# Two GpSimd sums for the first FFN's gate vector are written into the first mixer's second half

## The chip, the cores and the metric

The kernel runs on one core of one Trainium2 chip. The metric is the device time of one execution in microseconds (us); with several runs, their median. The engines are TensorE (PE, matrix products; PEld is its weight load), VectorE (DVE), ScalarE (ACT), GpSimd (POOL) and SyncE (SP, which here issues the loads). Each works through its own queue in order and waits on semaphores for the others.

## The reference

Two layers on 512 tokens of 1024 values. Layer 0 mixes tokens with HGRN2, layer 1 with dilated attention; behind each mixer stands a SwiGLU FFN with 2816 inner columns. Six vectors per layer, computed from the condition c, scale, shift and gate:

```python
cond = jax.nn.silu(c)
for layer in range(DEPTH):
    mod = (cond @ ada_w[layer] + ada_b[layer])[:, None, :]
    sh1, sc1, g1, sh2, sc2, g2 = jnp.split(mod, 6, axis=-1)
    u = rms_norm(h, norm_g[layer, 0]) * (1.0 + sc1) + sh1
    y = hgrn2_mixer(u, ...) if layer % 2 == 0 else dilated_attention_mixer(u, ...)
    h = h + (1.0 + g1) * rms_norm(y, norm_g[layer, 1])
    u = rms_norm(h, norm_g[layer, 2]) * (1.0 + sc2) + sh2
    y = swiglu_ffn(u, ffn_w_in[layer], ffn_w_out[layer])
    h = h + (1.0 + g2) * rms_norm(y, norm_g[layer, 3])
```

The change concerns g2 of layer 0, called (0, 5) in the kernel: 1024 sums over 1024 products of cond and ada_w.

## The kernel before, in words

All large products are computed in float32 as three products of rounded parts: an operand is split into a high part (ACT, `hi`, `oh`, `uh`) and a low part (the rest, DVE or POOL, `lo`, `ol`, `ul`), and L419 to L421 multiply high by high, low by high and high by low into a PSUM bank (`three`).

**The stream of loads.** A list `items` holds every weight tile in the order of use, and between them the pieces of the six vectors. `Stream` loads them with SP into two rotating places (`raw`), and `process_to` and `pieces` (L70 to L107) split weight tiles into `hi` and `lo`. An item of the kind "do" loads nothing; its function is called when the stream comes to it.

**The gate vector (0, 5).** Its four load items stand among the four tiles of the first mixer's output weights (`early`, L363). For each half of 512 columns DVE multiplies the rows by cond and adds them up partition by partition into a place in `shared` (L243, L245, `ada_chunk`). What remains is a sum over the 128 partitions that leaves the result on all of them. POOL does it with `partition_all_reduce`; for (0, 5) that is L254 in `reduce_both`, a "do" item behind the third tile of the FFN's input weights (L366). Then `row_fin` (L299, L300) adds the bias and multiplies by the norm's weights into `gate`, which is read at the very end of the FFN.

**Where the order comes from.** Inside `with tc.manual_schedule` the engines take their instructions in the order in which they are written. Outside of it a scheduler with a timeline model orders them. The "do" item is processed outside, so the scheduler chose its place: both sums stand in POOL's queue among the last two heads of the HGRN2 mixer, each ahead of an `orr`.

**The end of the HGRN2 mixer.** For each of 8 heads, `core_c` computes the head's output on PE, ACT squares and sums it (`oss`), DVE adds a constant (`rv`, L436), POOL takes the power -0.5 (`orr`, L437), and DVE scales the head with it (`aT`, L1438). `core_d` transposes it on PE (`ps_a`, L1445, four matmuls), ACT copies it out (`oT_late`, L1446), and DVE multiplies it by the mixer's gate (L1456). `mixer_out` then splits it (`cut`, L415 and L416) and multiplies it by the output weights: first columns 0 to 511 for all four token tiles (banks `ps_mm`, heads 0 to 7 in turn), then columns 512 to 1023 one token tile at a time (banks `ps_a`). All this is still ordered by the scheduler for layer 0.

**The second half of `mixer_out`** is written out by hand. Per token tile: squares of y (L457), the reciprocal root on POOL (`rr`, L472), the update of h, the norm, transposes (L502), the FFN's input u (`u_of`) and its two parts (`parts_of`, L519 and L520; the low part mostly on POOL). The last of them is `n.parts_of(3, 1, dve)`. Meanwhile PE multiplies the early tokens by the first FFN weights (`half`), and then the late ones (L691, L694).

**Then `ffn(0)`.** DVE builds sums over tokens (L732 to L739), PE multiplies the next column block, and `seven_products` computes two column blocks at a time with seven quarter products. It loads quarters of the weights, splits three of them (`spare` for the even steps, `hiq`/`loq` for others, L767 and L771), adds quarters (L775 on POOL, L779 and L783 on DVE) and splits the sums (L791 and L795). The first quarter loads go to the two places that the gate's bias and norm rows leave free when L300 has read them.

Of the kernel before, what the change touches and what calls it, by code (L numbers as in the profile page):

```python
# [15 lines left out]
P = 128  # L16
# [135 lines left out]
def block_kernel(tc, x, c, positions, ada_w, ada_b, norm_g, hgrn_w_in, lower, hgrn_norm_g, hgrn_w_out,  # L152
                 attn_w_in, attn_w_out, ffn_w_in, ffn_w_out, inv_freq, out):
    nc = tc.nc
    act, dve, pool, pe = nc.scalar, nc.vector, nc.gpsimd, nc.tensor
# [3 lines left out]
    with ExitStack() as ctx:  # L159
# [10 lines left out]
        def fresh(p, shape, tag, bufs=1, dt=F32):  # L170
            uid[0] += 1
            return p.tile(shape, dt, name=f"{tag}{uid[0]}", tag=tag, bufs=bufs)
# [30 lines left out]
        accs = {}  # L203
# [45 lines left out]

        def reduce_both(l, v):  # L250

            def run(_):
                for hf in range(2):
                    pool.partition_all_reduce(accs[l, v, hf], accs[l, v, hf], P, bass.bass_isa.ReduceOp.add)  # L254
            return ("do", None, run)

        def ada_item(l, v, hf, kq):
            src = ada_w[l, kq * 512:(kq + 1) * 512, v * D + hf * 512:v * D + (hf + 1) * 512]
# [82 lines left out]
        items = []  # L341
# [21 lines left out]
        early = [ada_item(0, 5, hf, kq) for hf in range(2) for kq in range(2)]  # L363
        items += hg_o[:2] + early[:2] + hg_o[2:3] + early[2:] + hg_o[3:]
        f0a, f0b = ffn_ws(0)
        items += f0a[:3] + [reduce_both(0, 5)] + f0a[3:4] + [fin_item(0, 5, 0), fin_item(0, 5, 1)] + f0a[4:]  # L366
        items += weave(f0b[:9], ada_seq((1, 1), (1, 0)), 0, 0.9) + f0b[9:]
        AW = attn_w_in[0]

# [44 lines left out]
        def split(hi, lo, src):  # L414
            act.copy(hi, src)  # L415
            dve.tensor_sub(lo, src, hi.bitcast(F32))  # L416
# [109 lines left out]
        def mixer_out(oT, otp, groups, gate, l, side, close, tail=None):  # L526


            aux = ExitStack()
            oh, ol = [], []  # L530

            def parts(n):
                uid[0] += 1
                pp = aux.enter_context(tc.tile_pool(name=f"parts{uid[0]}", bufs=1, side=bass.opposite_side(side)))
                place = not oh
                for _ in range(n):
                    oh.append(fresh(pp, [P, S], f"oh{len(oh)}", 1, F32R))
                if place:
                    pp.tile([P, 72], F32, name=f"pad{uid[0]}")

            def cut(kt):
                ol.append(fresh(otp, [P, S], *(("oT", 7) if kt < 7 else ("oT_late", 2)), F32R))
                split(oh[kt], ol[kt], oT[kt])

            parts(groups[0])
            y0 = [bank("mm") for _ in range(NT)]
            y1 = {}

            def prods(y, t, kt, w):
                tok = slice(t * P, (t + 1) * P)  # L550
                c = slice((kt % 4) * 512, (kt % 4 + 1) * 512)
                three(y, oh[kt][:, tok], ol[kt][:, tok], w[0][:, c], w[1][:, c], kt == 0, kt == KT - 1)

            def mm(t, kts):
                if t not in y1:
                    y1[t] = bank("a")
                for kt in kts:
                    prods(y1[t], t, kt, ws[kt // 4])

            if tail is None:  # L560
                for kt in range(KT):
                    if kt % 4 == 0:
                        w = st.take()
                    cut(kt)
                    for t in range(NT):
                        prods(y0[t], t, kt, w)
                ws = [st.take(1), st.take(0)]
            else:
                with tc.manual_schedule(engines=ORDERED):
                    for kt in range(3):  # L570
                        cut(kt)
                    for kt in range(KT):
                        if kt % 4 == 0:
                            w = st.take(0)
                        if kt == KT - 1:
                            ws = [st.take(0), st.take(0)]
                            mm(0, range(7))
                        for t in range(NT):
                            prods(y0[t], t, kt, w)
                        if kt == 0:  # L580
                            for fn in tail[-1]:
                                fn()
                            parts(groups[1])
                        if kt < 4:
                            cut(kt + 3)
                        for fn in tail.get(kt, ()):
                            fn()
                        if kt == 6:
                            cut(7)
                        if kt in (4, 5):  # L590
                            for hi_f, lo_f in st.pieces(2, True):
                                hi_f()
                                lo_f()
                            st.fill()
            close()
            n = Turn(side, y0, y1, gate, (l, 1))

            with tc.manual_schedule(engines=ORDERED):
                (hi_a, lo_a), (hi_b, lo_b) = st.pieces(2)
                n.sq_y(0, 0)  # L600
                n.gated(0, 0)
                mm(0, range(8) if tail is None else (7,))
                n.sq_y(0, 1)
                n.gated(0, 1)
                n.r_y(0)
                n.sq_y(1, 0)
                n.gated(1, 0)
                n.sq_y(2, 0)
                n.upds(0)
                n.sq_y(3, 0)  # L610
                n.gated(2, 0)
                n.r_h(0)
                hi_a()
                n.xn(0)
                mm(1, range(8))
                n.sq_y(1, 1)
                n.gated(1, 1)
                n.r_y(1)
                n.gated(3, 0)
                hi_b()  # L620
                n.upds(1)
                lo_a()
                mm(2, range(4))
                n.flip(0, [bank("b"), bank("b")])
                n.u_of(0, 0)
                n.r_h(1)
                n.u_of(0, 1)
                n.parts_of(0, 0)
                n.xn(1)
                n.parts_of(0, 1)  # L630
                lo_b()
                st.fill()
                mm(3, range(4))
                (hi_a, lo_a), (hi_b, lo_b) = st.pieces(2)
                mm(2, range(4, 6))
                n.flip(1, [bank("b"), bank("b")])
                n.u_of(1, 0)
                n.u_of(1, 1)
                n.parts_of(1, 0)
                n.parts_of(1, 1, dve)  # L640
                mm(2, range(6, 8))
                n.sq_y(2, 1)
                n.gated(2, 1)
                n.r_y(2)
                hi_a()
                n.upd(2, 0)
                mm(3, range(4, 8))
                n.sq_y(3, 1)
                n.sq_h(2, 0)
                n.upd(2, 1)  # L650
                n.sq_h(2, 1)
                hi_b()
                n.gated(3, 1)
                n.r_y(3)
                n.r_h(2)
                lo_a()
                n.xn(2)
                fw = [st.take(0), st.take(0)]
                pss = [bank("mm") for _ in range(4)]

                def half(i, tok):
                    block(*fw[i // 2], (i % 2) * P, 256, pss[i], tok, fu)
                half(0, EARLY)
                half(1, EARLY)
                n.flip(2, [bank("b"), bank("b")])
                n.upds(3)
                n.u_of(2, 0)
                n.u_of(2, 1, (0, 1))
                n.r_h(3)
                n.u_of(2, 1, (2, 3))  # L670
                n.xn(3)
                n.parts_of(2, 0)
                n.parts_of(2, 1)
                lo_b()
                st.fill()
                half(2, EARLY)
                n.flip(3, [bank("b"), bank("b")])
                n.u_of(3, 0)
                n.u_of(3, 1)
                n.parts_of(3, 0)  # L680
                n.parts_of(3, 1, dve)
                half(3, EARLY)
                for hi_f, lo_f in st.pieces(2):
                    hi_f()
                    lo_f()
                st.fill()
                tok = LATE
                for kt in range(KT):
                    a = kt * 256
                    for m, w in enumerate(fw[0]):  # L690
                        pe.matmul(pss[0][:, tok], w[:, a:a + P], fuh[kt // 4][:, kt % 4, tok], start=kt + m == 0, stop=False)  # L691
                for kt in range(KT):
                    a = kt * 256
                    pe.matmul(pss[0][:, tok], fw[0][0][:, a:a + P], ful[kt // 4][:, kt % 4, tok], start=False, stop=kt == KT - 1)  # L694
                for i in range(1, 4):
                    half(i, LATE)
            aux.close()
            return pss
# [1060 lines left out]
```

## Time and profile before

| | |
|---|---|
| median of 3 runs | 1526.21 us (1524.55 to 1527.09) |
| the profiled execution | 1527.45 us |
| its span in the profile | 1525.7 us |
| PE busy | 1502.3 us, 98% |
| DVE busy | 1033.1 us, 68% |
| ACT busy | 694.2 us, 45% |
| POOL busy | 240.6 us, 16% |
| mean granted clock of PE | 0.993 |
| L254 on POOL (the two sums) | 2 instructions of 3.25 us |

Times in rows are microseconds from the start of the span; a row of a timeline gives start, duration, engine, line, operation, output and inputs, and in brackets how long the engine stood idle before it and what it waited for. A wait put down to "issue" is one for which no semaphore accounts. The granted clock is the share of full speed at which PE ran in a stretch.

### The profile page before, as it was taken

To read this page: it belongs to the slowest core of one execution; us is meant where nothing else is said; L and a number is where in the kernel's file an instruction comes from. 1 tells how busy PE (TensorE), PEld (TensorE's weight loads), DVE (VectorE), ACT (ScalarE), POOL (GpSimd) and SP (SyncE) were. 2 spreads that over 40 slices of the span, in tenths; PEclk is the share of its full clock that TensorE was granted. 3 is DMA by queue.
4 is the path that set the end of the run, shared out by engine and by line. 5 is a ranking of instruction groups with operands and counts; after the bars stand their busy time and mean duration, and the time that the engine had idled before them with its cause. 6 is when DMAs were issued, how large, how long until landed. Compare 5 with 4: busy or idle time off the path is not lost.

```text
span 1525.7 us, 23115 instructions
## 1 busy us (share of the span) xinstructions
PE 1502.3 (98%) x9111; PEld 1327.7 (87%) x9111; DVE 1033.1 (68%) x1764; ACT 694.2 (45%) x1107; POOL 240.6 (16%) x212
## 2 busy tenths in 40 slices
PE   8999999899999999999999999999999999999998
PEld 6777888689999988889888888988888999999886
DVE  4577767478888897473557686345656978888633
ACT  4443433174444443363366655236555634454231
POOL 1011211130222211040010111000002212221100
PEclk9999999899999999999999999999999999999999
DMA  9553444313343356415544533443202233334531
GB/s 305 160 185 127 161 141 166 111 56 111 111 111 111 111 186 235 140 54 149 154 126 125 139 111 111 138 111 84 84 29 83 84 104 107 107 107 158 194 110 56
DMA packets 207645, 192.83 MB, mean 126 GB/s; under 512 B 6776, under 2 KB 166704, under 8 KB 207536
## 3 DMA queue, kind: packets, MB, share of 16 engines
q1 hardware_dynamic: 206000, 190.87, 40.6%
q8 instruction: 71, 1.16, 0.3%
q0 software_dynamic: 1024, 0.13, 0.2%
q10 hardware_dynamic: 512, 0.35, 0.1%
q14 instruction: 38, 0.31, 0.1%
HBM read 189.17 MB, written 2.16 MB: 125 GB/s over the span
## 4 chain that ended last, share of the span: by engine, by line
PE 89%; issue 3%; DVE 3%; DMA 2%; ACT 2%; POOL 1%; POOLq 0%; DVEq 0%; ACTq 0%
PE ps_mm L419 19%; PE ps_mm L421 19%; PE ps_mm L420 19%; PE ps_b L419 3%; PE ps_b L420 3%; PE ps_b L421 3%; PE ps_a L419 3%; PE ps_a L420 3%; PE ps_a L421 3%; PE ps_mm L1165 2%; DMA raw<-in_ada_w_dram 1%; PE ps_a L1165 1%; PE ps_a L1610 1%; PE ps_a L1592 1%; PE ps_mm L223 1%
## 5 line engine op out<-in xcount | busy, mean ns | idle before, releaser
L419 PE MATMUL ps_mm<-uh,hi 128*128 128x512 f32 (+1 forms) x784 | 290.0, 370 | 0.0
L421 PE MATMUL ps_mm<-uh,lo 128*128 128x512 f32 (+1 forms) x784 | 288.7, 368 | 0.0
L420 PE MATMUL ps_mm<-ul,hi 128*128 128x512 f32 (+1 forms) x784 | 287.5, 367 | 0.0
L85 DVE TENSOR_TENSOR lo<-raw,hi 128x2048 fp32r<-128x2048 f32 x74 | 177.4, 2397 | 158.5 <-ACT hi L84 158.5
L84 ACT CAST hi<-raw 128x2048 fp32r<-128x2048 f32 x74 | 141.2, 1908 | 143.8 <-DMA raw<-in_ffn_w_out_dram 49.7
L419 PEld LDWEIGHTS ps_mm<-uh,hi 128*128 128x128 f32 x784 | 147.4, 188 | 31.6 <-issue 8.4
L421 PEld LDWEIGHTS ps_mm<-uh,lo 128*128 128x128 f32 x784 | 147.7, 188 | 23.4
L420 PEld LDWEIGHTS ps_mm<-ul,hi 128*128 128x128 f32 x784 | 147.5, 188 | 22.7
L791 ACT CAST hiq<-raw 128x1024 fp32r<-128x1024 f32 x72 | 72.3, 1051 | 72.1 <-DVE raw L779 70.7
L419 PE MATMUL ps_mm<-hi,oh 128*128 128x512 f32 x240 | 94.1, 392 | 0.0
L420 PE MATMUL ps_mm<-lo,oh 128*128 128x512 f32 x240 | 93.5, 390 | 0.0
L245 DVE SCALAR_TENSOR_TENSOR shared<-raw,cond,shared 128x512 f32<-128x512 f32 x98 | 73.3, 748 | 25.6 <-DMA raw<-in_ada_w_dram 23.9
L795 DVE TENSOR_TENSOR loq<-raw,hiq 128x1024 fp32r<-128x1024 f32 x72 | 84.9, 1218 | 0.0
L247 POOL PARTITION_ALL_REDUCE shared<-shared x12 | 39.9, 3322 | 239.6 <-DVE shared L245 239.6
L421 PE MATMUL ps_mm<-hi,ul 128*128 128x512 f32 x192 | 76.0, 396 | 0.0
L775 POOL TENSOR_TENSOR raw<-raw 128x512 f32<-128x512 f32 x36 | 57.9, 1607 | 114.6 <-DVE loq L771 45.7
L420 PE MATMUL ps_mm<-lo,uh 128*128 128x512 f32 x192 | 75.9, 395 | 0.0
L419 PE MATMUL ps_mm<-hi,uh 128*128 128x512 f32 x192 | 74.6, 396 | 0.0
L779 DVE TENSOR_TENSOR raw<-raw 128x1024 f32<-128x1024 f32 x36 | 44.1, 1225 | 40.9 <-POOL raw L775 40.9
L421 PE MATMUL ps_mm<-hi,ol 128*128 128x512 f32 x176 | 68.5, 389 | 0.0
L419 PE MATMUL ps_a<-hi,oh 128*128 128x512 f32 x152 | 60.7, 400 | 0.0
L825 POOL TENSOR_TENSOR shared<-shared 128x256 f32<-128x256 f32 x36 | 27.7, 768 | 206.3 <-DVE shared L824 206.3
(403 smaller groups left out, 3939.6 us busy)
## 6 DMA issues: line engine op xcount, KB each, us to landing
raw<-in_ada_w_dram SPq DMA_DIRECT2D x40, 1024.0 KB, 5.1
raw<-in_ffn_w_in_dram SPq DMA_DIRECT2D x144, 256.0 KB, 4.2
raw<-in_attn_w_in_dram SPq DMA_DIRECT2D x48, 512.0 KB, 5.2
raw<-in_ffn_w_out_dram SPq DMA_DIRECT2D x22, 1024.0 KB, 4.9
raw<-in_hgrn_w_in_dram SPq DMA_DIRECT2D x12, 1024.0 KB, 5.5
raw<-in_attn_w_in_dram SPq DMA_DIRECT2D x12, 1024.0 KB, 5.0
raw<-in_ffn_w_in_dram SPq DMA_DIRECT2D x8, 1024.0 KB, 5.0
first<-in_ada_w_dram SPq DMA_DIRECT2D x14, 512.0 KB, 7.4
```

What stands on the lines that cost most here:

```text
L84: self.nc.scalar.copy(hi, t)
L85: self.nc.vector.tensor_sub(lo, t, hi.bitcast(F32))
L245: dve.scalar_tensor_tensor(a, r[:, k], sc, a, op0=OP.mult, op1=OP.add)
L247: pool.partition_all_reduce(a, a, P, bass.bass_isa.ReduceOp.add)
L419: pe.matmul(ps, ah, bh, start=start, stop=False)
L420: pe.matmul(ps, ah, bl, start=False, stop=False)
L421: pe.matmul(ps, al, bh, start=False, stop=stop)
L775: pool.tensor_add(r[:, 2], r[:, 2], r[:, 0])
L779: dve.tensor_tensor(r[:, 0:2], r[:, 0:3:2], r[:, 1:2].broadcast_to((P, 2, 512)), op=OP.add)
L791: act.copy(hi, src)
L795: dve.tensor_sub(lo, src, hi.bitcast(F32))
L1165: pe.matmul(vbanks[hf, t], a, w, start=e == 0 and which == 0, stop=e == KT - 1 and which == 2)
```

## The change

`reduce_both` no longer returns a "do" item but issues its two sums at once, and it is called inside the hand-written second half of `mixer_out`, behind `n.parts_of(3, 1, dve)`; the condition holds in layer 0 alone. The item leaves the list of loads. The same sums are computed on the same data.

```diff
         def reduce_both(l, v):
 
-            def run(_):
-                for hf in range(2):
-                    pool.partition_all_reduce(accs[l, v, hf], accs[l, v, hf], P, bass.bass_isa.ReduceOp.add)
-            return ("do", None, run)
+            for hf in range(2):
+                pool.partition_all_reduce(accs[l, v, hf], accs[l, v, hf], P, bass.bass_isa.ReduceOp.add)
...
-        items += f0a[:3] + [reduce_both(0, 5)] + f0a[3:4] + [fin_item(0, 5, 0), fin_item(0, 5, 1)] + f0a[4:]
+        items += f0a[:4] + [fin_item(0, 5, 0), fin_item(0, 5, 1)] + f0a[4:]
...
                 n.parts_of(3, 0)
                 n.parts_of(3, 1, dve)
+                if (l, 5, 1) in accs:
+                    reduce_both(l, 5)
                 half(3, EARLY)
```

The instructions of each engine stay the same in number, but for POOL, which has 4 changes of configuration around the two sums before and 2 now. Apart from the names' numbers the order changes on POOL, and, by the scheduler, at the end of the HGRN2 mixer on DVE and PE. SP's and ACT's orders stay.

POOL at the end of the HGRN2 mixer, before (`ISA shared` is a sum, `ISA` alone a change of configuration, `rr` the first root of the mixer's second half):

```order
L1387 TENSOR_TENSOR q_2129<-qd_2107,fpre_2113 128x512
L254 ISA
L254 ISA shared<-shared 128x512
L437 ISA
L437 TENSOR_TENSOR orr_2297<-rv_2298,expo 128x4
L254 ISA
L254 ISA shared<-shared 128x512
L437 ISA
L437 TENSOR_TENSOR orr_2331<-rv_2332,expo 128x4
L472 TENSOR_TENSOR rr_2564<-rv_2562,expo 128x1
```

POOL at the change from `mixer_out` to the FFN, now (line numbers of the changed file; `ul` is the last low part, `raw` the first sum of weight quarters):

```order
L518 TENSOR_TENSOR ul<-u_2904,uh 128x4x128
L253 ISA
L253 ISA shared<-shared 128x512 x2
L775 ISA
L775 TENSOR_TENSOR raw_3098<-raw_3098 128x512
```

Both sums have gone from ahead of the two orr to between ul and the first raw, where nothing stood before; the two orr now follow q directly.

DVE at the last head of the HGRN2 mixer, before and now (`lo` is the low part of the last tile of output weights, `aT` the scaled last head):

```order
L416 TENSOR_TENSOR oT_2491<-oT_late_689,oh_2358 128x512
L85 TENSOR_TENSOR lo_2456<-raw_2447,hi_2455 128x2048
L1438 TENSOR_TENSOR aT_2325<-ps_b_2317,orr_2331 128x512
L1456 TENSOR_TENSOR oT_late_690<-oT_late_690,Q_2280 128x512
```

```order
L414 TENSOR_TENSOR oT_2491<-oT_late_689,oh_2358 128x512
L1438 TENSOR_TENSOR aT_2325<-ps_b_2317,orr_2331 128x512
L85 TENSOR_TENSOR lo_2456<-raw_2447,hi_2455 128x2048
L1456 TENSOR_TENSOR oT_late_690<-oT_late_690,Q_2280 128x512
```

The scaled head has moved ahead of the low part.

PE at the same place, before and now (`ident,aT` are the four transposes; the rows with oh_2358 belong to head 6; the banks ps_mm hold columns 0 to 511, ps_a_2533 the other columns of the first token tile):

```order
L420 MATMUL ps_mm_2364<-lo_2189,oh_2358 128x512
L421 MATMUL ps_mm_2364<-hi_2188,oT_2491 128x512
L1445 MATMUL ps_a_2336<-ident,aT_2325 128x128 x4
L419 MATMUL ps_a_2533<-hi_2377,oh_2352 128x512
L420 MATMUL ps_a_2533<-lo_2378,oh_2352 128x512
```

```order
L417 MATMUL ps_mm_2361<-hi_2188,oh_2358 128x512
L418 MATMUL ps_mm_2361<-lo_2189,oh_2358 128x512
L1445 MATMUL ps_a_2336<-ident,aT_2325 128x128 x4
L419 MATMUL ps_mm_2361<-hi_2188,oT_2491 128x512
L417 MATMUL ps_mm_2362<-hi_2188,oh_2358 128x512
```

The transposes have moved ten matmuls ahead, into the products of head 6. Behind them now come 10 matmuls to ps_mm and 19 to ps_a_2533, and then the first product with the last head; before, it was 21 to ps_a_2533.

## The prediction

> **What bounds the kernel now.** I read the page first, then the waits of TensorE (PE), then the chain of waits around the place where the two sums over partitions run, then the timelines of GpSimd (POOL), VectorE (DVE) and PE there, and last the stretch into which the sums move.
>
> ```profile
> span 1525.7 us, 23115 instructions
> PE 1502.3 (98%) x9111; PEld 1327.7 (87%) x9111; DVE 1033.1 (68%) x1764; ACT 694.2 (45%) x1107; POOL 240.6 (16%) x212
> ```
>
> PE is busy for 98% of the span, so the time is PE's work plus the few moments in which it stands still. An edit on GpSimd can change the time only if it removes or makes such a moment. The waits of PE name the longest:
>
> ```profile
> PE ps_a L1445 <- DVE aT L1438: 6.3, 1, 6.3
> PE ps_b L502 <- DVE xn L496: 2.5, 2, 1.6
> ```
>
> It is one wait of 6.3 us: the transposes of the last head (L1445) wait for DVE's scaled head aT (L1438). The chain of waits says what DVE waited for:
>
> ```profile
> 278.34 0.75 DVE shared L245
> 279.10 0.61 DVE oT_late L1456
> 279.73 0.63 ACT oh L415
> 280.38 0.70 DVE oT L416
> 281.08 0.81 issue
> 281.89 3.25 POOL shared L254
> 285.22 7.26 issue
> 292.48 1.06 POOL orr L437
> 293.56 0.70 DVE aT L1438
> 294.31 1.12 PE ps_a L1445 x4
> ```
>
> DVE's aT needs the factor orr, which POOL computes in 1.06 us (L437). Ahead of it in POOL's queue stands one of the sums (L254), and between the sum's end and orr lie 7.26 us in which no semaphore is waited for. POOL's timeline, and the entries of its sequencer for L437 and L254, show what those are:
>
> ```profile
> 260.32 3.25 POOL L254 PARTITION_ALL_REDUCE shared<-shared  x1 [21.98 <-DVE shared L245]
> 272.12 1.06 POOL L437 TENSOR_TENSOR orr<-rv,expo 128x4 f32<-128x4 f32 x1 [8.55 <-DVE rv L436]
> 281.89 3.25 POOL L254 PARTITION_ALL_REDUCE shared<-shared  x1 [8.70 <-DVE oT L416]
> 292.48 1.05 POOL L437 TENSOR_TENSOR orr<-rv,expo 128x4 f32<-128x4 f32 x1 [7.34 <-issue]
> ```
> ```profile
> L254 POOLq MODIFY_POOL_CONFIG  x4: 9/10/11, 238.3 to 273.4; - x4
> L437 POOLq MODIFY_POOL_CONFIG  x4: 98/98/98, 263.5 to 285.1; - x4
> ```
>
> Before each sum and before each orr behind it, POOL's sequencer changes its configuration. The change at 273.4 us is followed by the sum at 281.89, the one at 285.1 by orr at 292.48: 8.5 and 7.4 us until the first instruction of the new kind. The 8.5 is an upper bound, since the sum's last input ends at 279.09 us (278.34 + 0.75); the 7.4 is a price, since orr's input was there:
>
> ```profile
> 279.61 0.17 DVE L436 TENSOR_SCALAR rv<-oss 128x4 f32<-128x4 f32 x1
> 280.38 0.69 DVE L416 TENSOR_TENSOR oT<-oT_late,oh 128x512 fp32r<-128x512 f32 x1 [0.60 <-ACT oh L415]
> 282.19 4.08 DVE L85 TENSOR_TENSOR lo<-raw,hi 128x2048 fp32r<-128x2048 f32 x1 [1.12 <-ACT hi L84]
> ```
>
> orr's input rv was done at 279.78 us. Orr started 12.7 us later.
>
> **What the change removes.** Both sums and their four configuration changes leave the place ahead of the two orr. The first sum costs nothing where it is: the orr behind it waited for its own input (the row at 272.12 names DVE rv). The second is the one above. Without it orr runs from about 279.9 to 281.0. In the new order DVE has aT directly behind the 0.69 us at 280.38, so aT is done at about 281.8. PE has the four transposes ten matmuls sooner than before. What PE and its clock do around the old wait:
>
> ```profile
> 294.31 1.12 PE L1445 MATMUL ps_a<-ident,aT 128*128 128x128 f32 x4 [6.28 <-DVE aT L1438]
> 288.03:294.31 6.28, 0.00 (x1) 0.00 (x1) 0.69 (x1) 0.00 (x0) 1.05 (x1) 0.66 0.44 150
> 294.31:300.33 6.02, 6.02 (x16) 4.88 (x17) 1.39 (x2) 1.30 (x2) 0.00 (x0) 0.50 0.00 0
> 300.33:305.98 5.65, 5.65 (x26) 4.66 (x25) 0.07 (x1) 0.69 (x2) 0.00 (x0) 1.00 0.01 3
> ```
>
> The first row is PE's timeline, the others are the table of stretches (PE busy and count, PEld, DVE, ACT, POOL, then the granted clock, DMA share, GB/s). A matmul of 512 columns at full clock takes 5.65 / 26 = 0.217 us here, so ten take 2.2 us, and PE comes to the transposes at 288.03 - 2.2 = 285.8 us, 4 us behind the time at which aT is ready. The wait of 6.28 us goes completely.
>
> With it goes a second cost. Behind the wait PE runs 6.02 us at a granted clock of 0.50 and does in them 4 transposes and 12 matmuls, half of what full clock does: 6.02 x 0.50 = 3.0 us lost. The Trainium skill, "TensorE: Matmul & The Clock Gate", Part 1, says that the array drops to half clock after an idle window of some 3.4 us and is back after about 3.4 us of work. By that figure the loss would be 3.4 x 0.5 = 1.7 us and the sum 8.0 instead of 9.3; the trace shows the half clock, but over 6.02 us, and I take the trace.
>
> What is late next? The transposes' result goes through ACT, DVE, ACT, DVE before the products with the last head:
>
> ```profile
> 295.46 0.69 ACT L1446 ACTIVATE oT_late<-ps_a,smallB 128x512 f32<-128x512 f32 x1 [13.30 <-PE ps_a L1445]
> 297.56 0.69 DVE L416 TENSOR_TENSOR oT_late<-oT_late,oh 128x512 fp32r<-128x512 f32 x1 [0.68 <-ACT oh L415]
> ```
>
> From 295.43 (the transposes' end) to 298.25 that takes 2.8 us. The new order puts 10 + 19 matmuls between the transposes and the first product with the last head, 29 x 0.217 = 6.3 us. Covered. The low part of the last output weight (282.19, 4.08 us) now comes behind aT and ends by 286.3 as before at the latest; the products that need it come 22 matmuls behind the transposes, after 290. Covered. From 306 us on, the chain runs over the norm of each token tile and starts from PE's results, so it moves as a whole.
>
> **What the change adds.** The sums now stand behind the last GpSimd subtraction (ul, L520), with one configuration change ahead of them and one behind; then comes the first sum of weight quarters (L775). POOL there, and the instructions of DVE and PE that could be late:
>
> ```profile
> 334.88 4.41 POOL L520 TENSOR_TENSOR ul<-u,uh 128x512 fp32r<-128x512 f32 x3 [1.19 <-ACT uh L519]
> 364.50 1.29 POOL L775 TENSOR_TENSOR raw<-raw 128x512 f32<-128x512 f32 x1 [25.22 <-DMA raw<-in_ffn_w_in_dram]
> ```
> ```profile
> 347.89 2.29 DVE L85 TENSOR_TENSOR lo<-raw,hi 128x2048 fp32r<-128x2048 f32 x1
> 351.83 0.69 DVE L299 TENSOR_TENSOR gate<-shared,raw 128x512 f32<-128x512 f32 x1
> 354.16 0.69 DVE L299 TENSOR_TENSOR gate<-shared,raw 128x512 f32<-128x512 f32 x1
> 362.67 1.76 DVE L771 TENSOR_TENSOR spare<-raw,spare 128x1536 fp32r<-128x1536 f32 x1 [0.93 <-ACT spare L767]
> 368.17 2.43 DVE L795 TENSOR_TENSOR loq<-raw,hiq 128x1024 fp32r<-128x1024 f32 x2
> ```
> ```profile
> 371.77 0.28 PE L419 MATMUL ps_mm<-uh,spare 128*128 128x256 f32 x1
> 376.17 0.28 PE L421 MATMUL ps_mm<-sums,loq 128*128 128x256 f32 x1
> ```
>
> In the times of the old trace (in the new one all of it about 9 us earlier): POOL is free at 339.29, has its configuration at 347.8 (+8.5), ends the sums at 351.05 and 354.3 (3.25 each), and is back at 361.7 (+7.4). Its next work started at 364.50, when a DMA had landed: 2.8 us to spare. The first gate addition at 351.83 finds its sum done; the second, at 354.16, waits 0.15 us. Queued behind it on DVE are the second halves of the gate, which free the places that the first two quarter loads go to, and the sums over tokens.
>
> The dearer part is DVE beside the sums. The low part at 282.19 took 4.08 us, the same shape at 347.89 2.29: 1.79 us lost over the 2.95 us (282.19 to 285.14) beside the sum, a share of 0.61. DVE is busy nearly throughout 348 to 354.3, so two sums cost it up to 6.5 x 0.61 = 4.0 us. The lower bound is near nothing: the masking of a head's scores, which reads PSUM, ran beside the first sum in its usual 0.68 us, and DVE's first products with the gate's input read PSUM too:
>
> ```profile
> 260.27 0.68 DVE L1404 TENSOR_TENSOR aT<-ps_a,causal 128x512 f32<-128x512 f32 x1
> ```
>
> I take the upper one, since most of what stands there has the shape of the low part. The delay passes on to the quarter loads and to spare and loq. The low half in spare was done at 364.43 and first used after 371.77: 7.3 us to spare; the first loq was done at about 369.4 and is used at 376.17: 6.8 us. So 4.0 us are hidden, and I cost the addition at nothing; if that cover were gone, each further microsecond would be one of PE.
>
> The Trainium skill speaks against this place: "SBUF — State Buffer", section "SBUF: two separate sides", says that a GpSimd instruction and a DVE instruction with two SBUF inputs lock their shared ports for a whole instruction, and that the loser is blocked completely. By it DVE would lose the full 6.5 us. The row of 4.08 us shows 61% of the overlap lost, not all.
>
> **Sum.** 6.28 + 3.0 = 9.3 us less, nothing added. The profiled execution took 1527.45 us, 1.75 more than its span, and becomes 1518.15; it stands 1.24 above the median of the runs (1526.21), which becomes 1516.9.
>
> **Rivals.** (a) A part is given back: DVE is blocked for all of the 6.5 us beside the sums, and the quarter loads, freed later, land up to 3 us later still; 9.5 us are 2.7 more than the 6.8 to spare, and PE waits that long before loq. For it: DVE is nearly full there. Against: the share of 0.61. Time 1516.9 + 2.7 = 1519.6; chance 0.12. (b) The change frees nothing: the scheduler's other moves, or another input of aT, keep PE waiting until about 294. Against it: the other input of aT (the head's products and rv) was there at 279.78, and no other instruction stands ahead of orr in the new order. Time 1526; chance 0.04. (c) Slower: the configuration changes take far longer here, beside the quarter loads. If each took 18 us, the sums would end at 339.3 + 18 + 6.5 = 363.8, POOL would be back at 381.8, and its sum of quarters would end at 383.1 instead of 365.8, 17.3 us late. PE has 6.8 of those to spare, waits 10.5, and loses another 3.0 at half clock: 13.5 - 9.3 = 4.2 us slower, 1530.4. It decides from a delay of about 13 us on (6.8 + 6.3, since the half clock comes on top). Against it: 8.5 and 7.4 us in the rows, with DMA running at the same time. Chance 0.04.
>
> **Numbers.** The forecast holds 0.80 of the chance. A measurement of this kernel tells 0.2%, 3 us, from no change. Forecast and (a) are faster by more than that: 0.92; (b) 0.04; (c) 0.04. The three runs before spread over 2.5 us (1524.55 to 1527.09); the range lets the new median lie that far below the forecast, and above it as far as (a) and 0.8 us of spread: 1514.4 to 1520.4.
>
> **What would show it.** In the new profile: no wait of L1445 for aT; orr about 1 us long at 280; granted clock 1.00 from 285 to 306; the first norm's squares 9 us sooner; two sums back to back at about 339 and 342 us, 8 us behind the last ul; the low part beside them stretched; L775 at about 355, and no PE wait at the first spare or loq. A PE wait there over 2 us, or a half-clock stretch, would show the forecast wrong in that part; an unchanged start of the mixer's second half would show it wrong altogether.

## The result, and the profile after

The changed kernel took 1515.79 us (median of 6 runs, 1515.40 to 1518.16) against 1523.95 (6 runs, 1521.87 to 1527.09): a ratio of 0.9948, 95% interval 0.9934 to 0.9962, so 5.8 to 10.1 us less. Forecast were 9.3 us less and a range of 1514.4 to 1520.4. The first lines of the page and the longest waits of TensorE, after:

```profile
span 1513.7 us, 23113 instructions
PE 1497.8 (99%) x9111; PEld 1324.4 (87%) x9111; DVE 1032.8 (68%) x1764; ACT 692.5 (46%) x1107; POOL 245.0 (16%) x212
```
```profile
PE ps_b L500 <- DVE xn L494: 2.6, 2, 1.6
PE ps_mm L1103 <- DVE cols L1133: 2.2, 1, 2.2
```

The wait of the transposes for aT has gone, and no other has come. GpSimd's timeline, after:

```profile
276.95 1.01 POOL L435 TENSOR_TENSOR orr<-rv,expo 128x4 f32<-128x4 f32 x1 [6.73 <-DVE rv L434]
322.58 4.42 POOL L518 TENSOR_TENSOR ul<-u,uh 128x512 fp32r<-128x512 f32 x3 [1.18 <-ACT uh L517]
332.77 7.00 POOL L253 PARTITION_ALL_REDUCE shared<-shared  x2 [5.77 <-issue]
355.90 1.28 POOL L775 TENSOR_TENSOR raw<-raw 128x512 f32<-128x512 f32 x1 [16.13 <-DMA raw<-in_ffn_w_in_dram]
```

The last orr starts 0.14 us after its input (rv ends at 276.81) instead of 12.7. The sums stand 5.77 us behind the last ul, and L775 again waits for a DMA, not for GpSimd. VectorE at the last head, PE's transposes there, and a stretch of the output products behind them (the third number from the end, 1.00, is the granted clock):

```profile
276.65 0.16 DVE L434 TENSOR_SCALAR rv<-oss 128x4 f32<-128x4 f32 x1
277.42 0.69 DVE L414 TENSOR_TENSOR oT<-oT_late,oh 128x512 fp32r<-128x512 f32 x1 [0.61 <-ACT oh L413]
278.02 0.68 DVE L1438 TENSOR_TENSOR aT<-ps_b,orr 128x512 f32<-128x512 f32 x1
```
```profile
282.59 0.60 PE L1445 MATMUL ps_a<-ident,aT 128*128 128x128 f32 x4
```
```profile
282.75:293.64 10.89, 10.89 (x52) 9.08 (x50) 2.08 (x3) 2.00 (x4) 0.00 (x0) 1.00 0.29 96
```

aT is ready at 278.70, 3.9 us ahead of the transposes (the forecast: 4), and PE goes on at full clock.

**Where the 12 us between the two spans come from.** The two profiled executions are 12.0 us apart, more than the change can do. Three marks on PE tell why: the first product L1395 of the first head, long before anything moved; the first product L694 in the mixer's second half; the first product with a low quarter, spare. The marks of before and of after (the first spare of before stands in the prediction at 371.77):

```profile
114.14 0.38 PE L1395 MATMUL ps_a<-qd,ki 128*128 128x128 f32 x2
340.21 0.39 PE L694 MATMUL ps_mm<-ul,hi 128*128 128x256 f32 x2
```
```profile
111.12 0.38 PE L1395 MATMUL ps_a<-qd,ki 128*128 128x128 f32 x2
327.91 0.28 PE L694 MATMUL ps_mm<-ul,hi 128*128 128x256 f32 x1
359.47 0.28 PE L417 MATMUL ps_mm<-uh,spare 128*128 128x256 f32 x1
```

Of the 12.0 us, 3.0 arise ahead of the first mark. From the first mark to the second it is 226.07 before and 216.79 after: 9.28 us, all of the change. From the second to the third it is 31.56 both times, and from there to the end 1153.9 and 1154.2. So no cost of the new place shows on PE.

### The profile page after: what moved, and what is told of

Read it like the earlier page. It is cut to its first block, busy times and chain, and to the rows that moved or that the text cites. A ratio compares the mean times of both kernels' runs of the same rounds, so it can differ in the third digit from the quotient of the medians.

```text
span 1513.7 us, 23113 instructions
## 1 busy us (share of the span) xinstructions
PE 1497.8 (99%) x9111; PEld 1324.4 (87%) x9111; DVE 1032.8 (68%) x1764; ACT 692.5 (46%) x1107; POOL 245.0 (16%) x212
## 4 chain that ended last, share of the span: by engine, by line
PE 93%; issue 2%; ACT 1%; DVE 1%; POOL 1%; DMA 1%; POOLq 0%; DVEq 0%; ACTq 0%
PE ps_mm L417 20%; PE ps_mm L419 20%; PE ps_mm L418 20%; PE ps_b L417 3%; PE ps_b L419 3%; PE ps_b L418 3%; PE ps_a L417 3%; PE ps_a L419 3%; PE ps_a L418 3%; PE ps_mm L1165 1%; PE ps_a L1165 1%; PE ps_a L1610 1%; PE ps_a L1592 1%; PE ps_mm L223 1%; PE ps_a L1659 1%
## 5 line engine op out<-in xcount | busy, mean ns | idle before, releaser
L417 PEld LDWEIGHTS ps_mm<-uh,hi 128*128 128x128 f32 x784 | 147.4, 188 | 31.6 <-issue 8.4
L775 POOL TENSOR_TENSOR raw<-raw 128x512 f32<-128x512 f32 x36 | 57.9, 1608 | 105.4 <-DVE loq L771 45.7
```

Of the source, the lines that this page charges most:

```text
L417: pe.matmul(ps, ah, bh, start=start, stop=False)
L775: pool.tensor_add(r[:, 2], r[:, 2], r[:, 0])
```

## The experiments

The row of after is the result above (6 runs); all others were timed in five rounds beside runs of the kernel before. The marks of all profiles (A: first L1395 to first L694; B: to the first spare; C: to the end; us; the last column is the ratio to before with its 95% interval):

| kernel | first L1395 | A | B | C | time, us | ratio |
|---|---|---|---|---|---|---|
| before | 114.14 | 226.07 | 31.6 | 1153.9 | 1523.3 to 1524.1 | 1 |
| after | 111.12 | 216.79 | 31.6 | 1154.2 | 1515.79 | 0.9948 (0.9934 to 0.9962) |
| after_again | 111.21 | 216.76 | 31.6 | 1154.4 | 1515.50 | 0.9943 (0.9931 to 0.9955) |
| second_only | 111.60 | 216.74 | 31.6 | 1153.9 | 1515.03 | 0.9944 (0.9933 to 0.9956) |
| first_only | 111.54 | 223.90 | 31.6 | 1154.3 | 1523.07 | 0.9995 (0.9987 to 1.0004) |
| plain | 113.54 | 216.79 | 31.6 | 1154.5 | 1516.40 | 0.9952 (0.9940 to 0.9964) |
| double | 110.79 | 216.77 | 31.6 | 1159.7 | 1521.27 | 0.9989 (0.9980 to 0.9998) |
| triple | 110.84 | 216.78 | 31.6 | 1159.2 | 1518.33 | 0.9968 (0.9956 to 0.9981) |
| pause_short | 110.91 | 216.76 | 36.3 | 1153.8 | 1519.94 | 0.9982 (0.9973 to 0.9990) |
| pause_long | 112.82 | 216.77 | 41.8 | 1153.6 | 1526.25 | 1.0013 (1.0004 to 1.0022) |
| pause_long2 | 110.94 | 216.78 | 42.2 | 1153.6 | 1525.34 | 1.0012 (1.0004 to 1.0021) |
| pause_warm | 112.11 | 216.78 | 40.0 | 1154.6 | 1523.94 | 0.9999 (0.9988 to 1.0009) |

### The changed kernel again

> The changed kernel once more, beside the others. Every theory: about 9 us under before (6 to 11), no wait of the last head's transposes, granted clock 1.00 through the output products. If the 3 us by which the two profiles already differ ahead of the change belong to single executions, the start of the first value product will again scatter by about 3 us between profiles, with no link to the change.

The code is that of the changed kernel. It came out 8.6 us under before (1515.50 against 1524.12, 0.9943), and A is the same to 0.03 us. The first column of the table scatters from 110.79 to 114.14 us, over kernels that are alike up to there: the start-up differs by 3 us between executions, whatever the kernel.

### Which of the two sums

Theory: the second sum, with the configuration change behind it, was the whole cost. Rival: each sum bore a share.

```diff
-                    reduce_both(l, 5)
+                    reduce_one(l, 5, 1)
...
+        items += f0a[:3] + [reduce_item(0, 5, 0)] + f0a[3:4] + [fin_item(0, 5, 0), fin_item(0, 5, 1)] + f0a[4:]
```

> Only the sum of the second half of the columns moves to the new place; the first stays ahead of the last but one orr. Theory (the second sum and the configuration change behind it are the whole cost): as the changed kernel, 9 us under before, no wait of the transposes. Rival (each sum costs its share): about 4.5 us under before.

`reduce_one` issues one of the two sums, and `reduce_item` puts it into the stream as a "do" item, as before. For the other kernel the last arguments 1 and 0 are exchanged.

> Only the sum of the first half moves; the second stays ahead of the last orr. Theory: no gain, within 2 us of before, the wait of the transposes still about 6 us and about 6 us of half clock behind it. Rival (each sum costs its share): about 4.5 us under before.

second_only gains all (A 216.74), first_only nothing that the timing can tell (0.9995). The rival falls. GpSimd and PE's longest wait in first_only:

```profile
269.37 1.01 POOL L437 TENSOR_TENSOR orr<-rv,expo 128x4 f32<-128x4 f32 x1 [33.62 <-DVE rv L436]
278.27 3.25 POOL L252 PARTITION_ALL_REDUCE shared<-shared  x1 [7.89 <-DVE oT L416]
288.40 1.05 POOL L437 TENSOR_TENSOR orr<-rv,expo 128x4 f32<-128x4 f32 x1 [6.88 <-issue]
```
```profile
PE ps_a L1447 <- DVE aT L1440: 4.8, 1, 4.8
```

GpSimd's idle times ahead of the sum and ahead of the last orr are somewhat shorter here (7.9 and 6.9 us against 8.7 and 7.3), and A is 2.2 shorter than before: 1.5 by the wait (4.8 instead of 6.3), the rest by a shorter stretch at half clock behind it. That stretch in before, then in first_only (the second number behind the bounds is PE's busy time, all of it behind the wait):

```profile
290.07:300.31 10.24, 6.00 (x16) 4.88 (x17) 2.08 (x3) 1.30 (x2) 1.05 (x1) 0.50 0.06 19
```
```profile
287.90:294.73 6.83, 4.49 (x13) 3.72 (x14) 2.08 (x3) 1.31 (x2) 1.05 (x1) 0.50 0.00 0
```

Whether the missing first sum or the execution made the idle times shorter, one profile can't say.

### The sum or the change of configuration

```diff
+                if kq == 1 and (l, v, hf) == (0, 5, 1):
+                    b = a.unsqueeze(1).broadcast_to((P, 2, 512))
+                    pool.tensor_tensor(shared[:, 0:2], b, b, op=OP.add)
```

> The changed kernel with an extra GpSimd addition over 1024 columns (its result is not used) ahead of the last orr, where the second sum stood: about 2.6 us of GpSimd's ordinary kind, so without a change of configuration. Theory (the change of configuration is what makes the old place dear): orr ends at about 283, aT at 284, still ahead of the transposes at 286 (minus what the start saves), so as the changed kernel, 9 us under before. Rival (any GpSimd work of some 3 us ahead of orr stops TensorE, and cools its clock): 3 to 6 us under before.

```profile
278.45 2.28 POOL L248 TENSOR_TENSOR shared<-shared 128x1024 f32<-128x1024 f32 x1 [5.97 <-DVE shared L245]
280.90 1.32 POOL L438 TENSOR_TENSOR orr<-rv,expo 128x4 f32<-128x4 f32 x1 [0.17 <-DVE rv L437]
```

2.28 us of GpSimd's ordinary work ahead of the same orr cost nothing: A is 216.79, and the time is that of the changed kernel within its interval. Orr starts as soon as the addition is over, and aT comes in time:

```profile
282.25 0.69 DVE L1441 TENSOR_TENSOR aT<-ps_b,orr 128x512 f32<-128x512 f32 x1 [0.91 <-POOL orr L438]
```

It is done at 282.94, and PE comes to the transposes at 285.01. A sum of 3.25 us alone, 1.0 longer than the addition, would by this estimate have fitted too. So the dear thing at the old place was not that GpSimd was in use, but the changes of configuration around the sum: of the 12.7 us by which the old orr started late, 2.1 passed ahead of the sum, 3.25 in it, and 7.3 between it and orr.

### How much the new place can hide

```diff
                     reduce_both(l, 5)
+                    reduce_both(l, 5)
```

> The changed kernel with both sums done twice at the new place (the sum is taken again over 128 equal copies, so the gate vector comes out 128 times too large ahead of its bias). Four sums of 3.5 us there. Theory (the sums are hidden because VectorE's loss beside them, 4.2 us, fits into what is to spare): VectorE loses about 8.3 us, the first low part of the quarter sums comes about 1 us after TensorE wants it; 7 to 8 us under before, with a TensorE wait of 0.5 to 3 us there. Rival (the place has far more cover than that): as the changed kernel, 9 us under before and no wait. Rival (VectorE is blocked completely beside a sum): 14 us lost, a TensorE wait of 6 us or more with half clock behind it, no better than before.

The loss is greater than I expected: 1521.27 us is 2.1 us under before, not 7 to 8, and part C is 5.5 us longer (1159.7 against 1154.2). PE's new wait in it is not for loq:

```profile
PE ps_mm L417 <- DVE mid L902: 2.8, 2, 2.4
```

PE waits for VectorE's product mid of the second plain column block (L902, in the kernels before and after L901). That product reads the last PSUM banks of the block, and PE writes to them again in the fifth of the seven quarter products. Back in the traces of before and after, the product and PE's first write behind it (before, then after; L733 ahead of them is one of the instructions that run beside the sums in after):

```profile
346.76 1.22 DVE L733 TENSOR_TENSOR mid<-mid 128x1024 f32<-128x1024 f32 x1
372.42 0.69 DVE L901 TENSOR_TENSOR mid<-ps_mm,shared 128x512 f32<-128x512 f32 x1
```
```profile
377.30 0.28 PE L419 MATMUL ps_mm<-sums,hiq 128*128 128x256 f32 x1
```
```profile
333.33 3.27 DVE L106 TENSOR_TENSOR lo<-raw,hi 128x1024 fp32r<-128x1024 f32 x1
336.52 3.33 DVE L733 TENSOR_TENSOR mid<-mid 128x1024 f32<-128x1024 f32 x1
363.82 0.68 DVE L901 TENSOR_TENSOR mid<-ps_mm,shared 128x512 f32<-128x512 f32 x1
```
```profile
365.00 0.28 PE L417 MATMUL ps_mm<-sums,hiq 128*128 128x256 f32 x1
```

Before, the product was done at 373.11, 4.2 us ahead; after, at 364.50, 0.5 us ahead. In the changed kernel two VectorE instructions that take 1.22 us elsewhere take 3.27 and 3.33 beside the sums, 4.2 us lost, of which 3.7 reach this product. So the cover was 4.2 us and not 6.8, and 0.5 is left. A third sum tests it:

```diff
                     reduce_both(l, 5)
+                    pool.partition_all_reduce(accs[l, 5, 1], accs[l, 5, 1], P, bass.bass_isa.ReduceOp.add)
```

> The changed kernel with three sums at the new place (the second half is summed twice, so that half of the gate vector comes out 128 times too large ahead of its bias). Theory (behind the changed kernel's sums only about 0.5 us are left between VectorE's product for the second plain column block, which frees a PSUM bank, and TensorE's first write to that bank): VectorE loses about 2 us more than in the changed kernel, TensorE waits 1 to 2 us for that product, half clock may follow: 1 to 4 us above the changed kernel. Rival (the first use of the low quarter sums is what ends the cover, 3 us behind): as the changed kernel, no wait.

```profile
366.75 0.68 DVE L902 TENSOR_TENSOR mid<-ps_mm,shared 128x512 f32<-128x512 f32 x1
```
```profile
367.58 0.36 PE L417 MATMUL ps_mm<-sums,hiq 128*128 128x256 f32 x1 [2.36 <-DVE mid L902]
```
```profile
370.00:375.00 5.00, 5.00 (x39) 5.00 (x39) 4.90 (x7) 3.77 (x5) 0.73 (x1) 0.87 0.15 41
```

With three sums PE waits 2.36 us for that product, and part of the next 5 us runs at half clock; the kernel takes 1518.33, 2.5 above the changed kernel. The profiled execution is one of the slower ones (1520.13), with a part C 5.0 longer than that of after. The theory holds; the rival, that loq ends the cover, falls.

### What a pause of PE costs

Theory: the old wait cost its length and then a stretch of half clock. The changed kernel gets a made pause behind L694 in layer 0:

```diff
+                if l == 0:
+                    tb = bank("a")
+                    pe.matmul(tb[:, 0:P], ident, ident, start=True, stop=True)
+                    act.copy(shared[:, 0, 0:P], tb[:, 0:P])
+                    for k in range(7):
+                        act.copy(shared[:, (k + 1) % 2, 0:P], shared[:, k % 2, 0:P])
+                    pe.matmul(bank("a")[:, 0:P], shared[:, 7 % 2, 0:P], ident, start=True, stop=True)
                 for i in range(1, 4):
                     half(i, LATE)
```

> The changed kernel with a made pause of TensorE in the second half of the first mixer, between the late tokens of the first and the second column block: a product, 8 copies of 128 columns in a chain on ScalarE, and a product that reads the last copy (all of it extra work, the result not used). About 2.5 us of pause. Theory (a pause costs itself, and beyond some length half clock behind it): the pause alone, 2.5 us above the changed kernel, granted clock 1.00 behind it. Rival (the clock follows any pause): 1 us or more on top.

> The same with 23 copies, about 7 us of pause. Theory (the half clock behind the old wait was a cost of its own, about 3 us): 7 us for the pause and 2 to 3 us for a stretch of about 6 us at half clock behind it, 9 to 10 us above the changed kernel, about as slow as before. Rival (the half clock behind the old wait had another cause): 7 us above, granted clock 1.00.

The long pause has range(22). Stretches of 3 us from the start of the pause on, pause_short:

```profile
329.00:332.00 3.00, 0.34 (x1) 0.34 (x2) 3.00 (x4) 2.73 (x9) 0.00 (x0) 0.86 0.00 0
332.00:335.00 3.00, 3.00 (x17) 3.00 (x17) 3.00 (x3) 1.51 (x2) 2.62 (x1) 0.57 0.00 0
335.00:338.00 3.00, 3.00 (x28) 3.00 (x27) 3.00 (x2) 1.78 (x1) 3.00 (x2) 1.00 0.13 41
```

I was wrong on the short one, and the rival held: a wait of 2.66 us was followed by half clock for most of 3 us (17 matmuls where 28 fit), and B grew by 4.7, not by 2.7. The long one (wait 7.61) made B 10.3 longer, as the theory said. It was run once more (pause_long2) beside the last kernel, which fills the long pause with matmuls. The added lines stand between the copies and the product that reads the last copy:

```diff
+                    for k in range(35):
+                        pe.matmul(tb, fw[0][0][:, 0:P], fuh[0][:, 0, ALL], start=True, stop=True)
```

> The long pause once more, beside the next kernel: about 10 us above the changed kernel, 1 to 3 us above before, a wait of 7.6 us and half clock behind it.

> The long pause filled: 35 matmuls of 512 columns (7.6 us at full clock, their result not used) run while ScalarE copies. Theory (half clock is a cost of its own, which idling brings): granted clock 1.00 throughout, TensorE waits at most 0.5 us, and the kernel is 2 to 3 us faster than the long pause with the same delay, so some 7.5 us above the changed kernel. Rival (the delay alone costs): as the long pause.

The stretches behind the pause in pause_long2, and two stretches inside the filled one in pause_warm:

```profile
335.00:338.00 3.00, 1.35 (x6) 1.35 (x7) 3.00 (x2) 2.84 (x7) 3.00 (x2) 0.50 0.13 25
338.00:341.00 3.00, 3.00 (x16) 3.00 (x16) 2.96 (x3) 0.51 (x1) 1.56 (x1) 0.50 0.52 150
341.00:344.00 3.00, 3.00 (x24) 3.00 (x23) 3.00 (x4) 1.27 (x2) 0.00 (x0) 0.86 0.02 5
```
```profile
331.00:334.00 3.00, 3.00 (x15) 2.47 (x14) 3.00 (x3) 2.71 (x10) 0.24 (x1) 1.00 0.00 0
334.00:337.00 3.00, 3.00 (x15) 2.49 (x14) 3.00 (x2) 2.71 (x10) 3.00 (x1) 1.00 0.00 0
```

For much the same delay (8.09 us from the product ahead of the copies to the one behind, against 7.88 with the idle pause) PE stays at full clock when it has work, and B is 2.2 us shorter (40.0 against 42.2). By the granted clock the half speed behind the idle pause should cost 1.35 x 0.5 + 3.00 x 0.5 + 3.00 x 0.14 = 2.6 us, close to it. The times agree in direction only just: 1523.94 against 1525.34, 1.4 us where 2 to 3 were expected, ratios 0.9999 and 1.0012 with overlapping intervals. By the profiles, then, half clock is a cost of its own, of about 2 us; the timing alone wouldn't show it.

## Why the prediction was right, and where it was not

- **The wait and what caused it: right.** The wait of 6.28 us for aT went completely, and it was the second sum with its configuration changes (second_only, first_only, plain).
- **The half clock: right as a term of its own** (pause_warm), and 3.0 us right for the one execution that was profiled: 9.28 us went in part A, 9.3 were forecast. The fit is that close because the forecast and this comparison go by the same profiled execution of before; in another it would be another, for what the term is worth varies: in before PE ran 6.0 us at half clock behind a wait of 6.3, in first_only 4.5 behind 4.8, in pause_long2 about 5 us behind 7.6 and in pause_short about 3 behind 2.7. The timed medians, 8.2 and 8.6 us, agree with 9.3 within their intervals, and as well with the 8.0 that the prediction gives as the other sum.
- **The time: 1516.9 forecast, 1515.79 measured, closer than its parts.** The forecast started from a median of 1526.21 in three runs; in six it is 1523.95, 2.3 lower, while the gain of the medians is 1.1 smaller than forecast.
- **The first sum costs nothing where it stood: right within 2 us** (first_only: the interval reaches down to 0.9987, and A is 2.2 shorter in its one profile).
- **The configuration change at the new place: 5.77 us, not the upper bound of 8.5.** The ten other kernels with sums at the new place show 5.5 to 6.0 (triple 5.52, plain 6.03). The Trainium skill, "GPSIMD Engine Reference", section 2.1, "Instruction dispatch", gives about 6 us for the first call of newly loaded code, without an instruction in the profile; these rows agree. The change back, 7.3 us at the old place in before and 6.9 in first_only, is hidden at the new one by the DMA that L775 waits for.
- **VectorE's loss beside the sums: 4.2 us, forecast at most 4.0.** The share is 0.59 of the 7.00 us, as in the row from which it was taken (0.61). By the rule of the Trainium skill, "SBUF — State Buffer", section "SBUF: two separate sides", it would have been, by estimate, the full 7.0; the measurement decides.
- **The cover: wrong.** The step "the first loq was done at about 369.4 and is used at 376.17: 6.8 us" named the wrong end. I looked for the first uses of what VectorE writes, and not for the PSUM banks that its instructions give back. The first to come late is L901, with 4.2 us to spare, and 3.7 of these were used. The forecast of no cost at the new place held by 0.5 us, and that was luck: the cover that it counted on wasn't the one that held. Rival (a) had the right kind of loss with the wrong door; triple and double are what it looks like.
- **The span's 12.0 us:** 3.0 of them are start-up scatter. Read without the marks, the two profiles would have made the change a third larger than it is (12.0 against 9.28).

## What to carry to other kernels

On GpSimd a sum over partitions among ordinary instructions cost here its own 3.3 us, 5.5 us or more for the change of configuration ahead of it and about 7 for the one behind; put such sums together, and where nothing on GpSimd is waited for until both changes are over. For cover, look at the buffers that a delayed engine frees as well as at the data it makes. When two profiles differ by more than the change should do, find a mark ahead of it and one behind, and compare the stretch between.

## What the runs showed of the hardware that was not expected

A wait of PE of 2.66 us was enough for half clock behind it (pause_short, granted 0.57 in the next 3 us). The Trainium skill, "TensorE: Matmul & The Clock Gate", Part 1, speaks of an idle window of some 3.4 us and adds that the window runs freely; the second half would fit the varying lengths here, the first is not what this run shows. The waits of 2.4 us that were left over from too many sums were followed by half clock as well (granted 0.87 in triple's row above).

The traces show more. Stretches that are at half clock from end to end, each with granted 1.00 in the 3.41 us ahead of it and behind it, are these in pause_short, pause_long and pause_long2:

```profile
331.19:334.60 3.41, 2.94 (x13) 2.94 (x14) 3.41 (x3) 2.27 (x4) 2.22 (x1) 0.50 0.00 0
```
```profile
336.01:342.84 6.83, 4.32 (x20) 4.32 (x21) 6.80 (x4) 4.12 (x10) 5.42 (x2) 0.50 0.21 77
```
```profile
331.58:341.82 10.24, 5.17 (x24) 5.17 (x25) 10.21 (x7) 6.42 (x18) 7.00 (x2) 0.50 0.19 51
```

The lengths are 3.41 us and two and three times as much, and so are those of all others behind a wait: 10.24 in before, 6.83 in first_only, 3.41 in double and triple. pause_long and pause_long2 are the same code with the same wait of 7.61 us, and yet differ. So the moment at which a wait falls has a part in it, and not its length alone: in pause_long half clock begins 5.1 us into the wait, in pause_long2 2.5 us, in triple 0.4 us behind its end. What is left of the stretch when PE has work again is what it costs, by estimate half of 4.32 us in pause_long and half of 5.17 in pause_long2; the 0.4 us between the two is what B differs by (41.8 and 42.2). In every case PE had stood still for 2.0 us or more of the 3.41 us just ahead (2.04 in before, 2.19 in pause_short); in pause_long the 3.41 us one step earlier (329.19 to 332.60) hold 1.68 us of standstill, and the clock stayed at 1.00. No run was made to find how little is enough.

The start of the kernel, up to 111 or 114 us, differs by 3 us between executions. In the two traces of before and after the first 30 us already show it, with more matmuls and a higher clock in the latter; what decides it was not tried. The twelve profiles fall into two groups: before, plain and pause_long are at half clock for 6.83 us within the first 30 us and reach the first mark at 112.82 to 114.14; the others are so for 3.41 us or not at all, and reach it at 110.79 to 112.11. The two go together; which causes which is open.

```profile
0.00:30.00 30.00, 23.84 (x135) 18.84 (x135) 13.51 (x31) 14.45 (x25) 5.06 (x14) 0.89 1.01 306
```
```profile
0.00:30.00 30.00, 25.25 (x158) 19.59 (x159) 13.59 (x31) 14.98 (x26) 6.13 (x14) 0.94 1.01 306
```

Two sums directly behind one another take 7.0 us, and a third beside VectorE's work 5.3 us more, where one alone took 3.25.
